# A hybrid attention and mLSTM layer on one core: mLSTM gates, rotation, compressed products and convolution products in another order

## The chip, the core and the metric

The kernel runs as one program on one core of a Trainium2 chip. The metric is the time on the device in microseconds, the median over runs: lower is better. TensorE does the products, VectorE, ScalarE and GpSimd the rest; each engine takes its instructions strictly in its own order and waits for the others by semaphores.

## The reference

One decoder layer on 512 tokens of width 1024 in float32. After an RMS norm `h`, one product with `w_in` (1024 x 5408) gives the inputs of two token mixers. The part that matters here:

```python
z = h @ w_in
q_a, kc_a, vc_a, ks_a, vs_a, kw_a, vw_a, gate_a, qk_b, v_b, o_b, if_b, merge = split(z)
# attention: rotation of the first 16 of 64 components of q and k; three branches
out = concat([t1 * cos - t2 * sin, t2 * cos + t1 * sin, rest])          # partial_rope
kc, vc = compress(kc_a), compress(vc_a)      # 31 overlapping blocks of 32 tokens: gelu(flat @ w1) @ w2
o = g0 * attn(q, kc, vc) + g1 * attn(q, ks, vs) + g2 * attn(q, kw, vw)  # 8 heads, 2 key groups, causal
# mLSTM: convolution over 4 tokens and SiLU on q and k, gates i and f
qk = silu(b + sum_j w[j] * qk_b shifted by j)
lf = log_sigmoid(f);  bcum = cumsum(lf);  m = running maximum of (bcum[t] - bcum[s] + i[s])
h_t = (sum_s exp(bcum[t] - bcum[s] + i[s] - m) (q_t k_s) v_s) / max(|den|, exp(-m))
x = x + (sigmoid(g_a) * (y_a @ w_pa) + sigmoid(g_b) * (y_b @ w_pb)) @ w_out
```

A mixture of experts, a gated embedding and a last norm follow; the change does not touch them.

## The kernel before, in words

All products are split in float32r: a weight piece (128 x 1024, streamed by SyncE) is cast on ScalarE (`whWS`, L103), and the rest is taken on VectorE (`wlWS`, L106), which is the low split; TensorE then does the three products high by high, high by low and low by high. Inside the attention a piece is split at column 640: VectorE does 640, GpSimd 384 (L108); elsewhere VectorE does it all. The rows of a TensorE instruction are named `tp` for transposes, `mm`, `S` and `o` for products.

The stages ahead of the end, with the times of the profiled execution: norm and first products (0 to 38 us); the z1 stage (38 to 91 us), which makes queries, keys, values, gates (`gi`) and the compressed blocks; the attention (to 262 us), woven with the products of the mLSTM; then the mLSTM with the products of `merge` (L979, named z3 here), the output products and the experts.

In the z1 stage the list `ORDER` says in which order pieces come: z4 (288 columns: keys, values and all gates), z0 and z1 (queries), c0 and c1 (the compressed blocks' products, L623, of `bhl` with `w_ck1` and `w_cv1`). What must follow a piece is a generator (`z1_out`: rotate, split into `qs`, transpose at L544 into `qst`; `cmp_out`: gelu, second product). Generators stand in the list `later`, and `advance` steps each of them when its time (`WAIT`) is up. At the end, `while later: advance()` empties it. `cmp_in` makes the blocks' input: the sum `tb` (L614) and the split `bhl` (L615, L616), in two tiles of their own. `rope` (L505) has five VectorE operations: two products with `cos`, two with `nsin` and `sin`, one sum (L511 to L515).

After it come the mLSTM's gates (L733 to L793), some 40 VectorE operations on tiles of 4 to 128 columns: forget gates as a logarithm (ScalarE's table for Ln is loaded at L749), prefix sums by two products on TensorE (L763, L765), maxima by a scan between transposes, and the table `UB` of exponents.

Then the attention: `attention_steps` goes through 32 units (4 query blocks, 4 head pairs, 2 branches). `unit_a` does the scores (L875), the maximum on VectorE (L876), the exponential on ScalarE (L880), the scaling on GpSimd (L886). Two units later `unit_t` transposes (L896) and splits (`ph` L899, `pl` L900), and `unit_pv` multiplies with the values (L912, L917). `cmp_a` (L829) does the scores of the compressed blocks up to `pc` (L850), `cmp_b` its transposes (L857). Between these steps, `weave` takes from `z2_steps` as many products as `FILL_A` says for a query block: first eight channels of the convolution's q and k (24 products of 512 columns each, L802, with four VectorE operations each at L809 and L812), then four channels of v and o (96 products of 256 columns, L292). When these are used up, no more come before the mLSTM's stage.

Instructions are recorded in the order of the text, and a scheduler then sets the order on each engine; nothing is moved while it runs.

Of the kernel before, what the change touches and what calls it, by code (L numbers as in the profile page):

```python
# [19 lines left out]
P = 128  # L20
# [112 lines left out]
def tile_hybrid(ctx, tc, x, p, positions, g_mix, w_in, b_if, w_ck1, w_ck2, pe_ck, w_cv1, w_cv2, pe_cv,  # L133
# [186 lines left out]
    with tc.tile_pool(name="start", bufs=1) as sp:  # L320
# [58 lines left out]
        with in_order():  # L379
# [81 lines left out]
            A.activation(trig[:, 0:2], red.rearrange("p c (b j) -> p c b j", b=NB), AF.Sin)  # L461
            last_g = G.tensor_scalar(trig[:, 2], trig[:, 0], -1.0, None, op0=OP.mult)
# [14 lines left out]
        sin, cos, nsin = trig[:, 0], trig[:, 1], trig[:, 2]  # L477
# [131 lines left out]
    def cmp_in(kv):  # L609
        tb = zp.tile([P, 16, 62], F32, name="tb", bufs=1)  # L610
# [15 lines left out]
    def cmp_out(kv):  # L626

# [107 lines left out]
    with tc.tile_pool(name="gates", bufs=1) as gp:  # L735
        tri = gp.tile([P, 2, P], F32, name="tri")
# [24 lines left out]
        lf2 = lf.rearrange("p b h -> p (b h)")  # L761
        ps = PA.tile([P, 512], F32, name="tp")
# [63 lines left out]
    def attention_steps(ap):
# [135 lines left out]
    with tc.tile_pool(name="att", bufs=1) as ap:  # L962
        weave(attention_steps(ap), z2_steps(ap))
# [764 lines left out]
```

## Time and profile before

| | |
|---|---|
| median of 3 runs | 707.13 us (704.98 to 707.24) |
| profiled execution, its own time | 707.7 us |
| its span in the trace | 705.9 us |
| busy: TensorE, VectorE, ScalarE, GpSimd | 684.4, 561.5, 434.5, 139.1 us |
| granted clock of TensorE, mean | 0.998 |

Busy time of TensorE holds an instruction's whole length, while the next may have started; two starts in a row tell more of how fast it goes. Idle time in brackets stands with what ended it.

### The profile page before, as it was taken

What the parts mean: (1) busy time and instruction counts of PE and PEld (TensorE: products, weight loads), DVE (VectorE), ACT (ScalarE), POOL (GpSimd) and SP (SyncE); (2) the same over time, 40 slices, a digit from 0 to 9 for tenths busy, and PEclk for the clock granted to TensorE, in tenths of its full rate; (3) what the DMA queues carried; (4) which work ended last, traced back from release to release, by engine and by line L of the source; (5) the groups of instructions that cost most, each with busy time, mean ns of one, the idle gap of its engine ahead of it and who ended that gap; (6) DMA issues with size and microseconds to landing.
All of it is one profiled execution on the core that took longest, in us unless ns stands there. A gap on an engine that the chain in (4) does not pass through costs nothing.

```text
span 705.9 us, 11369 instructions
## 1 busy us (share of the span) xinstructions
PE 684.4 (97%) x3813; PEld 579.5 (82%) x3813; DVE 561.5 (80%) x1430; ACT 434.5 (62%) x848; POOL 139.1 (20%) x189
## 2 busy tenths in 40 slices
PE   8999989999999999999999999999999999999995
PEld 5889967789999998888888888876788888887784
DVE  5768988888768668878775763768999999986986
ACT  5547756576556765665453242236999999987642
POOL 5510033234334210000000002122222222110000
PEclk9999999999999999999999999999999999999999
DMA  8435631222212113232229348945999989507511
GB/s 290 110 96 151 168 100 37 84 61 61 61 31 59 32 40 82 61 91 64 86 63 354 121 124 284 372 150 189 384 386 374 370 299 364 234 30 265 194 61 61
DMA packets 81992, 113.72 MB, mean 161 GB/s; under 512 B 9417, under 2 KB 49945, under 8 KB 81930
## 3 DMA queue, kind: packets, MB, share of 16 engines
q1 hardware_dynamic: 72322, 97.14, 41.5%
q0 software_dynamic: 5648, 11.53, 4.5%
q10 hardware_dynamic: 3960, 4.29, 1.8%
q8 instruction: 31, 0.51, 0.3%
q14 instruction: 31, 0.25, 0.1%
HBM read 108.41 MB, written 12.58 MB: 171 GB/s over the span
## 4 chain that ended last, share of the span: by engine, by line
PE 74%; DVE 8%; DMA 7%; ACT 4%; issue 4%; POOL 3%; ACTq 0%; SPq 0%; POOLq 0%; DVEq 0%
PE S L1510 12%; PE mm L979 12%; PE mm L292 7%; PE mm L1682 6%; PE mm L1535 6%; PE mm L1151 6%; PE mm L802 3%; PE mm L1315 3%; PE tp L896 2%; DMA wr<-in_w_re 2%; PE S L875 2%; PE tp L1496 2%; DVE wlWS L106 2%; PE mm L912 1%; ACT whWS L103 1%
## 5 line engine op out<-in xcount | busy, mean ns | idle before, releaser
L106 DVE TENSOR_TENSOR wlWS<-rawWR,whWS 128x1024 fp32r<-128x1024 f32 (+3 forms) x75 | 85.9, 1153 | 25.5 <-ACT whWS L103 24.6
L103 ACT ACTIVATE whWS<-rawWR 128x1024 fp32r<-128x1024 f32 (+1 forms) x76 | 79.1, 1049 | 35.7 <-PE tp L1223 7.0
L106 DVE TENSOR_TENSOR wlWS<-rawWE,whWS 128x1024 fp32r<-128x1024 f32 x58 | 69.2, 1222 | 3.6 <-ACT whWS L103 2.3
L103 ACT ACTIVATE whWS<-rawWE 128x1024 fp32r<-128x1024 f32 x58 | 60.6, 1071 | 5.1 <-PE S L1510 4.1
L292 PE MATMUL mm<-wlWS,hTh 128*128 128x256 f32 (+1 forms) x184 | 54.2, 295 | 0.1
L292 PE MATMUL mm<-whWS,hTl 128*128 128x256 f32 (+1 forms) x184 | 54.2, 294 | 0.0
L292 PE MATMUL mm<-whWS,hTh 128*128 128x256 f32 (+1 forms) x184 | 53.9, 293 | 0.0
L979 PE MATMUL mm<-hTh,whWS 128*128 128x512 f32 x128 | 50.3, 393 | 0.0
L886 POOL TENSOR_SCALAR pr<-pr,sm 128x128 f32<-128x128 f32 (+3 forms) x64 | 34.7, 554 | 78.7 <-DVE sm L884 34.8
L979 PE MATMUL mm<-hTh,wlWS 128*128 128x512 f32 x128 | 50.0, 391 | 0.0
L979 PE MATMUL mm<-hTl,whWS 128*128 128x512 f32 x128 | 50.0, 391 | 0.0
L1510 PE MATMUL S<-whWS,tgh 128*128 128x512 f32 x120 | 48.6, 405 | 0.0
L1510 PE MATMUL S<-wlWS,tgh 128*128 128x512 f32 x120 | 47.8, 398 | 0.0
L1510 PE MATMUL S<-whWS,tgl 128*128 128x512 f32 x120 | 47.3, 395 | 0.0
L880 ACT ACTIVATE pr<-pr,sm 128x128 f32<-128x128 f32 (+3 forms) x64 | 35.4, 555 | 17.0 <-DVE sm L878 16.8
L899 ACT ACTIVATE ph<-tp 128x512 fp32r<-128x512 f32 (+1 forms) x48 | 25.1, 522 | 20.3 <-PE tp L896 19.8
L108 POOL TENSOR_TENSOR wlWS<-rawWR,whWS 128x384 fp32r<-128x384 f32 (+1 forms) x17 | 25.2, 1484 | 62.0 <-ACT whWS L103 57.1
L292 PEld LDWEIGHTS mm<-wlWS,hTh 128*128 128x128 f32 x184 | 34.9, 190 | 0.4 <-DVE wlWS L106 0.3
L292 PEld LDWEIGHTS mm<-whWS,hTl 128*128 128x128 f32 x184 | 34.9, 190 | 0.1
L292 PEld LDWEIGHTS mm<-whWS,hTh 128*128 128x128 f32 x184 | 34.9, 190 | 0.0
L1540 POOL DMA_INDIRECT y_dram<-ye,gidx x16 | 20.8, 1302 | 62.1 <-ACT aeh L1524 59.0
L876 DVE CUSTOM_DVE_ANT_0 pr<-S,strip 128x128 f32<-128x128 f32 (+3 forms) x64 | 29.3, 485 | 3.9 <-PE S L875 3.4
(492 smaller groups left out, 2076.8 us busy)
## 6 DMA issues: line engine op xcount, KB each, us to landing
rawWE<-in_w_e SPq DMA_DIRECT2D x59, 512.0 KB, 9.1
rawWR<-in_w_in SPq DMA_DIRECT2D x40, 512.0 KB, 3.9
mT<-in_w_e SPq DMA_DIRECT2D x22, 512.0 KB, 10.5
rawWR<-in_w_e SPq DMA_DIRECT2D x13, 512.0 KB, 10.1
rawWR<-in_w_out SPq DMA_DIRECT2D x8, 512.0 KB, 4.0
yy<-y_dram SPq DMA_DIRECT2D x8, 512.0 KB, 5.1
rawWR<-in_w_ck SPq DMA_DIRECT2D x4, 512.0 KB, 4.4
rawWR<-in_w_cv SPq DMA_DIRECT2D x4, 512.0 KB, 5.6
```

The costliest lines, as they stand in the source:

```text
L103: self.last_hi = self.nc.scalar.activation(h[:, :n], flat, AF.Copy)
L106: self.last = self.nc.vector.tensor_tensor(l[:, :c], flat[:, :c], h[:, :c].bitcast(F32), OP.subtract)
L108: self.nc.gpsimd.tensor_tensor(l[:, c:n], flat[:, c:], h[:, c:n].bitcast(F32), OP.subtract)
L292: T.matmul(dst[b], a[:, kk, b * P:(b + 1) * P], w[:, kk - k0, :n], start=(kk == 0 and i == 0 and b % share == 0), stop=(kk == NK - 1 and i ...
L876: V.tensor_tensor_reduce(pr[:, hh, :n], s_[:, :n], strip[:, 512 - q0:640], 0.125, -3.0e38, OP.add, OP.max, sm[:, 0, hh:hh + 1])
L880: A.activation(pr[:, hh, :n], pr[:, hh, :n], AF.Exp, bias=sm[:, 1, hh:hh + 1], accum_out=sm[:, 2, hh:hh + 1])
L886: G.tensor_scalar(pr[:, hh, :n], pr[:, hh, :n], sm[:, 3, hh:hh + 1], 1.0, op0=OP.mult, op1=OP.mult)
L979: T.matmul(ps, w[:, k], a[:, k], start=(k == 0 and i == 0), stop=(k == NK - 1 and i == 2))
L1151: T.matmul(ps, w[:, k, f * P:(f + 1) * P], a[:, k], start=(k == 0 and i == 0), stop=(k == 3 and i == 2))
L1510: T.matmul(ps, a[:, 2 * m + k], w[:, k], start=(m == 0 and k == 0 and i == 0), stop=(m == 3 and k == 1 and i == 2))
L1535: T.matmul(acc[c], a[:, k], w[:, 0, c * 512:(c + 1) * 512], start=(k == 0 and i == 0), stop=(k == 1 and i == 2))
L1682: T.matmul(acc, a[:, k], w[:, 0, lo:hi], start=(k == 0 and i == 0), stop=(k == NK - 1 and i == 2))
```

## The change

1. `ORDER`: the third piece of z4 comes before the first of c0, three pieces of c0 stand together, and z1 is last.
2. `rope`: a table `rot` holds cos twice and sin with both signs (four GpSimd operations); two products with it over 16 components and one sum of the swapped halves.
3. `bhl` and `tb` get no tiles of their own; they lie in the parts of `qst` and `oB` that are free so long. `w2d` is copied in `cmp_out`.
4. The convolution's pool is opened early, and `z2_steps` (`fill`) starts while `later` is emptied: seven steps (`FLUSH`) ahead of each step of a generator.
5. The gates are a generator of four steps, `gate_steps`, that `z2_steps` advances at every eighth step of the products of `vo` from the second channel on; `behind` ties each recorded instruction to the last one before it on its engine.
6. `cmp_b` comes one unit later.

```diff
-ORDER = "z4 z4 c0 z4 c0 c0 z0 c0 z0 c1 z1 c1 z1 c1 c1".split()
+ORDER = "z4 z4 z4 c0 c0 c0 z0 c0 z0 c1 z1 c1 c1 c1 z1".split()
+FLUSH = 7
...
     def rope(z, j, heads, pool):
...
-        V.tensor_tensor(a[..., 0:8], z[..., 0:8], tab(cos), OP.mult)
-        V.tensor_tensor(a[..., 8:16], z[..., 8:16], tab(cos), OP.mult)
-        V.tensor_tensor(b[..., 0:8], z[..., 8:16], tab(nsin), OP.mult)
-        V.tensor_tensor(b[..., 8:16], z[..., 0:8], tab(sin), OP.mult)
-        V.tensor_tensor(z[..., 0:16], a, b, OP.add)
+        for i in range(2):
+            V.tensor_tensor(ab[:, i].rearrange("p (b h e) -> p b h e", b=2, h=heads), v,
+                            rot[:, i, 2 * j:2 * j + 2, None, :].to_broadcast([P, 2, heads, 16]), OP.mult)
...
+        for q in range(1 if joint else 2):
+            to = v.rearrange("p b h e -> p (b h) e") if joint else v[:, q]
+            V.tensor_tensor(halves(to, 0), halves(c[:, 0, q], 0), halves(c[:, 1, q], 1), OP.add)
...
-    bhl = zp.tile([P, 16, P], F32R, name="bhl", bufs=1)
+    bhl = qst[:, 4:8].rearrange("p h (m n) -> p (h m) n", n=P)
...
-        tb = zp.tile([P, 16, 62], F32, name="tb", bufs=1)
+        tb = oB.rearrange("p b n -> p (b n)")[:, 0:992].rearrange("p (m n) -> p m n", n=62)
...
-    with tc.tile_pool(name="gates", bufs=1) as gp:
+    def gate_steps(gp):
+        room = gp.tile([P, S], F32, name="cy", bufs=2)
...
-                for _ in tok_mm_steps(dst, 4 * h, 4 * h + 4, wh, wl, 256, 2):
+                for n, _ in enumerate(tok_mm_steps(dst, 4 * h, 4 * h + 4, wh, wl, 256, 2)):
+                    if c and n % 8 == 0:
+                        with behind():
+                            next(gates, None)
                     yield
...
-    while later:
-        advance()
+    fill = z2_steps(conv)
+    while later:
+        for w in list(later):
+            for _ in range(FLUSH):
+                next(fill)
+            if next(w[1], later) is later:
+                later.remove(w)
...
-                    else:
-                        cmp_b(i)
                     yield FILL_C[br - 1]
+                elif pair == 1 and br == 1:
+                    cmp_b(i)
...
-        weave(attention_steps(ap), z2_steps(ap))
+        weave(attention_steps(ap), fill)
```

Three places in the order. VectorE around the low split of z0's first piece (before: the only `wlWS` row here; `khh` and `kll` are keys, `gi` the gates):

```order
108 L580 TENSOR_TENSOR v_461<-mm,v_461 128x2x64
109 L515 TENSOR_TENSOR kz<-rope_a,rope_b 128x4x16
110 L106 TENSOR_TENSOR wlWS<-rawWR,whWS 128x1024
111 L594 CAST khh_456<-tp 64x2x256 x2
112 L585 TENSOR_TENSOR qs<-kz,qs 128x2x2x64
113 L596 CAST kll_457<-tp 64x2x256 x2
114 L580 TENSOR_TENSOR v_461<-S,v_461 128x2x64
```

and after the change, where the row of the same split is the last one (L614 is now L640, L594 is L621, L596 is L623, L106 is L107):

```order
94 L640 TENSOR_TENSOR oB<-TT,cols 128x16x31 x2
95 L621 CAST khh_460<-tp 64x2x256 x2
96 L612 TENSOR_TENSOR qs<-kz,qs 128x2x2x64
97 L623 CAST kll_461<-tp 64x2x256 x2
98 L607 TENSOR_TENSOR v_465<-S,v_465 128x2x64
99 L529 TENSOR_TENSOR rope_ab<-kz,rot 128x64 x2
100 L697 TENSOR_SCALAR gi<-gi 128x4x24
101 L540 TENSOR_TENSOR kz<-rope_ab 128x4x16
102 L107 TENSOR_TENSOR wlWS<-rawWR,whWS 128x1024
```

The split stood ahead of the casts `khh` and `kll`; now it stands behind them, behind a rotation and behind the scaling of `gi`.

TensorE at the last transposes of the queries before (L544; L649 is the second product of the compressed blocks, L802 the convolution):

```order
414 L623 MATMUL o<-whWS,bhl 128x256
415 L623 MATMUL o<-wlWS,bhl 128x256
416 L649 MATMUL S<-gT,w2d 128x64 x2
417 L544 MATMUL tp<-ident,qs 128x128 x8
418 L802 MATMUL mm<-hTh,whWS 128x512
419 L802 MATMUL mm<-hTl,whWS 128x512
420 L544 MATMUL tp<-ident,qs 128x128 x4
421 L802 MATMUL mm<-hTh,wlWS 128x512
422 L544 MATMUL tp<-ident,qs 128x128 x4
423 L802 MATMUL mm<-hTh,whWS 128x512
424 L544 MATMUL tp<-ident,qs 128x128 x4
425 L802 MATMUL mm<-hTl,whWS 128x512
```

and after (L544 is now L571, L802 is L830):

```order
414 L307 MATMUL S<-wlWS,hTh 128x256
415 L571 MATMUL tp<-ident,qs 128x128 x8
416 L830 MATMUL mm<-hTh,whWS 128x512
417 L830 MATMUL mm<-hTl,whWS 128x512
418 L830 MATMUL mm<-hTh,wlWS 128x512
419 L571 MATMUL tp<-ident,qs 128x128 x4
420 L830 MATMUL mm<-hTh,whWS 128x512
421 L830 MATMUL mm<-hTl,whWS 128x512
422 L571 MATMUL tp<-ident,qs 128x128 x4
423 L830 MATMUL mm<-hTh,wlWS 128x512
424 L830 MATMUL mm<-hTh,whWS 128x512
```

The compressed products ahead of the transposes are gone from here, and convolution products stand between the transposes; 35 of them stand ahead of the first scores.

TensorE in the last steps of the attention before (L896 transposes, L912 products with values, L292 products of `vo`):

```order
1403 L912 MATMUL mm<-ph,v_460 128x256
1404 L912 MATMUL mm<-pl,v_460 128x256
1405 L912 MATMUL mm<-ph,v_460 128x256
1406 L912 MATMUL mm<-pl,v_460 128x256
1407 L896 MATMUL tp<-ident,pr 128x128 x4
1408 L292 MATMUL mm<-whWS,hTl 128x256
1409 L292 MATMUL mm<-wlWS,hTh 128x256
1410 L292 MATMUL mm<-whWS,hTh 128x256
1411 L292 MATMUL mm<-whWS,hTl 128x256
1412 L292 MATMUL mm<-wlWS,hTh 128x256
1413 L292 MATMUL mm<-whWS,hTh 128x256
```

and after (L896 is now L937, L912 is L953, L979 is L1021):

```order
1398 L937 MATMUL tp<-ident,pr 128x128 x4
1399 L953 MATMUL mm<-ph,v_464 128x256
1400 L1021 MATMUL mm<-hTh,whWS 128x512
1401 L953 MATMUL mm<-pl,v_464 128x256
1402 L953 MATMUL mm<-ph,v_464 128x256
1403 L953 MATMUL mm<-pl,v_464 128x256
1404 L937 MATMUL tp<-ident,pr 128x128 x4
1405 L953 MATMUL mm<-ph,v_464 128x256
1406 L1021 MATMUL mm<-hTl,whWS 128x512
1407 L953 MATMUL mm<-pl,v_464 128x256
1408 L953 MATMUL mm<-ph,v_464 128x256
```

The eight products of `vo` between a step's transposes and its neighbour's products are gone, and one product of z3 stands in a step.

## Rows read from the trace of the kernel before

**Rows 1.** The summary of the page: busy time, share of the span and instructions of each engine.
```profile
PE 684.4 (97%) x3813; PEld 579.5 (82%) x3813; DVE 561.5 (80%) x1430; ACT 434.5 (62%) x848; POOL 139.1 (20%) x189
```

**Rows 2.** The table by stage (stretch and its length in us, busy time of each engine with its instructions, TensorE's granted clock, DMA share, GB/s).
```profile
91.00:106.00 15.00, 14.12 (x82) 11.04 (x79) 13.15 (x49) 8.37 (x17) 3.94 (x2) 1.00 0.31 88
106.00:120.00 14.00, 13.21 (x75) 9.83 (x73) 12.96 (x59) 9.35 (x31) 4.46 (x10) 1.00 0.15 39
120.00:140.00 20.00, 18.68 (x103) 15.59 (x103) 16.47 (x54) 11.23 (x30) 6.33 (x12) 1.00 0.28 79
140.00:160.00 20.00, 20.00 (x117) 17.51 (x117) 17.37 (x54) 13.97 (x33) 7.97 (x11) 1.00 0.19 54
160.00:180.00 20.00, 19.66 (x145) 18.37 (x144) 18.23 (x53) 12.05 (x28) 8.01 (x11) 1.00 0.22 57
180.00:200.00 20.00, 20.00 (x164) 19.80 (x163) 13.03 (x47) 12.90 (x35) 5.60 (x9) 1.00 0.18 50
```

**Rows 3.** TensorE in order of time, three places of the z1 stage; columns: start us, us, engine, line, operation, out<-in (partitions x elements, type), count, and in brackets the idle time before with its releaser.
```profile
50.01 0.29 PE L292 MATMUL mm<-whWS,hTl 128*128 128x288 f32 x1
51.58 0.39 PE L623 MATMUL o<-whWS,bhl 128*128 128x256 f32 x1 [1.27 <-DVE bhl L616]
...
57.14 0.28 PE L292 MATMUL mm<-whWS,hTh 128*128 128x256 f32 x1
...
62.90 0.28 PE L623 MATMUL o<-whWS,bhl 128*128 128x256 f32 x1
63.44 0.39 PE L623 MATMUL o<-wlWS,bhl 128*128 128x256 f32 x1 [0.26 <-DVE wlWS L106]
...
64.50 0.28 PE L292 MATMUL mm<-whWS,hTl 128*128 128x256 f32 x1
64.91 0.39 PE L292 MATMUL mm<-wlWS,hTh 128*128 128x256 f32 x1
```

**Rows 4.** TensorE in order of time at the last transposes of the queries, at the first scores and at `cmp_b`; columns as in rows 3.
```profile
88.58 0.56 PE L649 MATMUL S<-gT,w2d 128*128 128x64 f32 x4
90.68 1.09 PE L544 MATMUL tp<-ident,qs 128*128 128x128 f32 x8 [1.55 <-DVE qst L549]
...
104.50 0.39 PE L802 MATMUL mm<-hTl,whWS 128*128 128x512 f32 x1
105.40 0.33 PE L875 MATMUL S<-khh,qst 128*128 128x128 f32 x1 [0.51 <-DVE sm L876]
...
137.52 0.39 PE L802 MATMUL mm<-hTl,whWS 128*128 128x512 f32 x1
138.85 0.44 PE L857 MATMUL tp<-ident,pc 128*128 128x128 f32 x2 [0.94 <-DVE pc L850]
```

**Rows 5.** VectorE in order of time around the low split of z0's first piece; columns as in rows 3.
```profile
55.92 1.21 DVE L106 TENSOR_TENSOR wlWS<-rawWR,whWS 128x1024 fp32r<-128x1024 f32 x1
57.15 1.28 DVE L594 CAST khh<-tp 64x512 fp32r<-64x512 f32 x2
58.47 0.42 DVE L585 TENSOR_TENSOR qs<-kz,qs 128x256 fp32r<-128x256 f32 x1
58.90 0.69 DVE L596 CAST kll<-tp 64x512 fp32r<-64x512 f32 x1
```

**Rows 6.** VectorE in order of time: a rotation operation (L511) alone, a part of a split, a rotation operation beside GpSimd's part of it; the first and the last of 22 gate operations; L850 twice. Columns as in rows 3.
```profile
85.52 0.22 DVE L511 TENSOR_TENSOR rope_a<-zt,trig 128x64 f32<-128x64 f32 x1
...
87.00 0.82 DVE L106 TENSOR_TENSOR wlWS<-rawWR,whWS 128x640 fp32r<-128x640 f32 x1 [0.53 <-ACT whWS L103]
87.75 1.05 DVE L511 TENSOR_TENSOR rope_a<-zt,trig 128x64 f32<-128x64 f32 x1
...
98.34 0.18 DVE L768 COPY bc<-tp 128x16 f32<-128x16 f32 x1 [0.48 <-PE tp L763]
...
103.06 0.17 DVE L787 TENSOR_TENSOR ct<-tp,mp 128x16 f32<-128x16 f32 x1
...
138.38 0.42 DVE L850 TENSOR_TENSOR pc<-pc,r 128x256 f32<-128x256 f32 x1
...
177.20 1.24 DVE L850 TENSOR_TENSOR pc<-pc,r 128x256 f32<-128x256 f32 x1
```

**Rows 7.** GpSimd in order of time: its parts of low splits; columns as in rows 3.
```profile
87.05 2.62 POOL L108 TENSOR_TENSOR wlWS<-rawWR,whWS 128x384 fp32r<-128x384 f32 x2 [31.21 <-ACT whWS L103]
...
176.51 1.65 POOL L108 TENSOR_TENSOR wlWS<-rawWR,whWS 128x384 fp32r<-128x384 f32 x1 [0.58 <-ACT whWS L103]
```

**Rows 8.** ScalarE in order of time: a load of its function table; columns as in rows 3.
```profile
94.45 1.28 ACT L635 ACT_TABLE_LOAD   x1
```

**Rows 9.** TensorE in order of time in the last steps of the attention (eight products of L292 from 259.17 to 260.08); columns as in rows 3.
```profile
258.81 0.60 PE L896 MATMUL tp<-ident,pr 128*128 128x128 f32 x4
259.17 0.36 PE L292 MATMUL mm<-whWS,hTl 128*128 128x256 f32 x1
...
260.08 0.28 PE L292 MATMUL mm<-wlWS,hTh 128*128 128x256 f32 x1
260.20 0.28 PE L912 MATMUL mm<-ph,v 128*128 128x256 f32 x1
```

**Rows 10.** ScalarE in the same step.
```profile
259.45 0.60 ACT L899 ACTIVATE ph<-tp 128x512 fp32r<-128x512 f32 x1 [1.27 <-PE tp L896]
```

**Rows 11.** VectorE in the same step.
```profile
260.08 0.69 DVE L900 TENSOR_TENSOR pl<-tp,ph 128x512 fp32r<-128x512 f32 x1 [1.18 <-ACT ph L899]
```

More of the change, by code (lines that the diff above doesn't have):

```diff
@@ L267, in in_order, with behind @@
             last[i.engine] = i
+    @contextmanager
+    def behind():
+        cur = nc.cur_bb
+        traced = cur.bb.instructions
+        n = len(traced)
+        last = {i.engine: i for i in traced}
+        yield
+        assert nc.cur_bb is cur
+        for i in traced[n:]:
+            if i.engine in last:
+                tc.add_manual_dep(i, last[i.engine].name, mybir.DependencyInfo(
+                    mybir.DependencyClass.NoSync, mybir.DependencyReason.DATA), reason="behind")
     ident = const.tile([P, P], F32, name="ident")
@@ L334, in tile_hybrid @@
         bif = const.tile([P, 8], F32, name="bif")
+        rot = const.tile([P, 2, NB, 16], F32, name="rot")
         def square(b):
@@ L460, in tile_hybrid @@
             z4w.append(st.get(("z", 4, 1)))
-            A.activation(trig[:, 0:2], red.rearrange("p c (b j) -> p c b j", b=NB), AF.Sin)
-            last_g = G.tensor_scalar(trig[:, 2], trig[:, 0], -1.0, None, op0=OP.mult)
+            A.activation(trig, red, AF.Sin)
+            tr4 = trig.rearrange("p c (b j) -> p c b j", b=NB)
+            for s_ in range(2):
+                G.tensor_copy(rot[:, 0, :, 8 * s_:8 * s_ + 8], tr4[:, 1])
+                last_g = G.tensor_scalar(rot[:, 1, :, 8 * s_:8 * s_ + 8], tr4[:, 0], (1.0, -1.0)[s_], None, op0=OP.mult)
             zz_mm(3, 0, (0, 2, 1))
@@ L626, in cmp_out @@
     def cmp_out(kv):
+        if kv == 0:
+            V.tensor_copy(w2d, w2s[:, 0, :, None, :].to_broadcast([P, 2, 2, 64]))
         u = zp.tile([P, 256], F32, name="gelu_u", bufs=1)[:62]
@@ L734, in tile_hybrid @@
     UB = const.tile([P, 4, NB, NB], F32, name="UB")
-    with tc.tile_pool(name="gates", bufs=1) as gp:
-        tri = gp.tile([P, 2, P], F32, name="tri")
+    def gate_steps(gp):
+        room = gp.tile([P, S], F32, name="cy", bufs=2)
+        tri = room[:, 0:2 * P].rearrange("p (a b) -> p a b", a=2)
         G.memset(tri, 1.0)
@@ L761, in tile_hybrid @@
         lf2 = lf.rearrange("p b h -> p (b h)")
+        yield
         ps = PA.tile([P, 512], F32, name="tp")
@@ L769, in tile_hybrid @@
         V.tensor_tensor(u0, fi[:, :, 0:4], bc, OP.subtract)
+        yield
         ps3 = PA.tile([P, 512], F32, name="tp")
         T.transpose(ps3[:16, :P], u0.rearrange("p b h -> p (b h)"), ident)
-        ut = gp.tile([16, P], F32, name="ut")
+        ut = room[:16, 2 * P:3 * P]
         V.tensor_copy(ut, ps3[:16, :P])
-        cm = gp.tile([16, P], F32, name="cm")
+        cm = room[:16, 3 * P:]
         V.tensor_tensor_scan(cm, ut, ut, -3.0e38, OP.max, OP.max)
+        yield
         ps4 = PA.tile([P, 512], F32, name="tp")
@@ L796, in z2_steps @@
     def z2_steps(wp):
+        gates = gate_steps(wp)
         for c in range(8):
@@ L824, in z2_steps @@
                              AF.Copy if c < 2 else AF.Tanh, scale=1.0 if c < 2 else 0.5)
+    fill = z2_steps(conv)
[5 more added lines that the diff above has]
+                later.remove(w)
+    zp_c.__exit__(None, None, None)
+    tt_ctx.__exit__(None, None, None)
     def attention_steps(ap):
```

19 lines of the change are left out of this document (10 added, 9 removed).

## The prediction

> **What bounds the kernel now.** I read the summary first, then the table by stage, then TensorE's own rows in order of time where it stalls, then the engines it waits for. TensorE is busy 97% of the span [rows 1]. In the table by stage it is without a gap at 140-160 us and at 180-200 us; its idle time near this change lies ahead of that, and at 91-140 us VectorE is nearly as full as TensorE [rows 2]. Busy time hides part of the loss: a 256-column product shows 0.28 us, but the next one starts 0.12 us later. So I count stalls from start to start. The large ones are: 50.01 to 51.58 before the first compressed product, which waits for `bhl`; 62.90 to 63.44 and 64.50 to 64.91, which wait for a low split [rows 3]; 88.58 to 90.68 before the queries' transposes; 104.50 to 105.40 at the first scores; 137.52 to 138.85 before the transposes of `cmp_b` [rows 4]. Behind the attention, at 262 us, the products of z3 stand ready, so I let what is lost or won before it reach the end whole. 0.3% of this kernel is 2.1 us, about what a measurement of it can tell from no change. No large product is added or taken away: TensorE's work is the same, and the question is only where it stands still.
>
> **1. Compressed products later, the queries' first piece behind them.** In the order after, 13 products of z4 and 8 transposes stand between the place of the first stall and the first compressed product. By the old rows `bhl` came at 51.5, and those 21 pieces last beyond it. So the stall goes, 1.57 less a usual step of 0.13: -1.44. The pieces from the stall to z0 (8, 13, 8 and 16 of them) took from 51.58 to 57.14 [rows 3], 5.56 us, and they are the same ones after the change; TensorE now begins them at 50.13 and stands at z0's first piece at 55.7. The low split of this piece, which VectorE began at 55.92 and ended at 57.13 [rows 5], is now queued behind two casts `khh` (1.28), one `qs` (0.4), two casts `kll` (1.3), a `v`, a rotation and the scaling of `gi` (0.6 together, at the lengths of their kind): 3.6 us later, an end at 60.7. TensorE has 1.0 us of work that needs no low split (four products, four transposes, one compressed product) and would idle from 56.7 to 60.7. So the new wait lies between 0 (if the casts' inputs come much sooner) and 4.0 (the plain sum); I take **+3.0**, nearer the plain sum, since the order is fixed and only its start can move. Behind it four splits stand together ahead of TensorE, so the two later stalls go: -0.42 and -0.29. The step in all: +0.85 (from -2.15 to +1.85).
>
> **2. Convolution products between the transposes, rotation in three operations.** The stall at 88.58 is 2.10 us, of which the four small products take some 0.4: 1.7 lost. The transposes wait for `qst`, which on VectorE stands behind two rotation operations, the first of 1.05 us where such a one takes 0.22 [rows 6]; meanwhile GpSimd did its parts of two splits, 1.31 us each [rows 7]. In the order after, these two splits are whole on VectorE: +0.4 us each there (1.21 against 0.82 [rows 5, 6]), but GpSimd is out of the way, the rotation has three operations, and TensorE has 3, 2, 16 and 7 products of 0.23 us between the transposes and 7 behind them. So I take the 1.7 as gone. The stall at 104.50 (0.90 less a step of 0.23) goes too, since the 22 gate operations which VectorE did between 98.34 and 103.23 with a few others among them [rows 6] no longer stand ahead of the first scores. Between the two, gaps of 0.2 to 0.4 stand among the transposes; I take 1.4 us for these, since VectorE has 1.85 us to spare of 15 there now [rows 2] and the gate operations' 3.5 (22 of about 0.16) more after. Step: **-3.8** (from -1.7, the first stall alone, to -4.5).
>
> **3. Early attention.** At 106-120 us VectorE is busy 12.96 of 14 us, and TensorE idles 2.1 us at 106-140 [rows 2]. The convolution's first channel is done earlier, and so are VectorE's operations for it; the transposes of `cmp_b` come a unit later, which frees 1.33 less 0.23, 1.1 us. With some 1.3 of the small gaps: **-2.4** (from 0, if other waits fill the place, to -3.5).
>
> **4. Gates in the attention.** Some 40 small VectorE operations (the 22 in 3.5 us, and 17 of 0.17 ahead of them: about 6.3 us), and the two table loads (1.28 us for one [rows 8]), now fall into about 17 us at the change from the second to the third query block. There the convolution is over in the order after. By the nearest stretch of old without it, 180-200, VectorE would have 5.9 us free in 17; by 160-180, the same query blocks, 1.5 [rows 2]. So it lacks between 0.4 and 4.8 us. ScalarE has room for the loads (12 to 14 of 20 busy). A unit's result is needed two units later, which covers most of a lack that is made up soon: **+1.1** (0 to +4). `pc` takes 0.42 us alone and 1.24 while GpSimd's split of 1.65 us runs [rows 6, 7], like the rotation in step 2. [...]
>
> **5. A tail without fill.** Thirty-five products are used early, so those of `vo` run out between the last two pairs of scores. The last seven transpose steps of the attention have three products of z3 among them, where each had 6 to 8 products of 0.12 us. Such a step is 0.36 us of transposes (258.81 to 259.17) and 0.48 of products on TensorE [rows 9], 0.84 in all. But the transposes of a step stand behind the products of the step two before, and these behind a chain: transposes 0.60, `ph` 0.60, `pl` 0.69, products 0.48 [rows 9 to 11], 2.4 us for two steps, 1.2 for one. Seven times 0.36 is 2.5, less 0.7 for the three z3 products of 0.23: **+1.8** (0.5, if a chain overlaps the next one better than that, to 4.5, if the scores' own chain of reduction, exponential and scaling ends last).
>
> Sum: 0.85 - 3.8 - 2.4 + 1.1 + 1.8 = -2.45. The profiled execution took 707.7 us (span 705.9), 0.6 over the median of 707.13 of the runs shown. Against its own time the sum gives 705.25, against the median **704.7**.
>
> **The rivals.**
> *Gates and tail cost more than the transposes give (slower).* One mechanism: VectorE is late in the middle of the attention. Its price: each of GpSimd's splits in the stretch holds a two-input operation 0.8 us longer (1.24 against 0.42 [rows 6]), three of them 2.4 us; as VectorE has none to spare, TensorE waits, and step 4 is its upper end, +4; the tail, where VectorE's chain is again last, is +3.5. The sum is then +2.15: 709.3. It decides once VectorE is behind by more than the lead of two units, some 5 us. For it: the rows of 1.24 and 1.05. Against: most gate operations are short, and no TensorE work waits for them at once. Chance 0.24.
> *The new waits are covered (much faster).* The low split of z0 is there when TensorE comes, and the tail costs 1.0: -2.45 - 3.0 - 0.8 = -6.25, 700.9. For it: the split was just in time before. Against: its place in the order. Chance 0.15.
> *The stalls only change place (no change).* VectorE's work is the same but for some 2 us of rotation; step 3 gives nothing, and the sum is about 0: 707. The moved copy `w2d` does nothing at all, for it stands in the same early place in both orders. For it: VectorE is full around every stall [rows 2]. Chance 0.21.
>
> **How the numbers follow.** My forecast has 0.40, with 702.5 to 706.5 as its own range. Faster by over 0.3%: the second rival 0.15, the forecast's part below 705.0, 0.27, and 0.03 of the third: 0.45. Slower: the first rival but for 0.03, and 0.01 of the third: 0.22. Within 0.3%: the rest, 0.33. The range takes in the second rival's time with 1 us below it and the first's with 1 us above: 699.9 to 710.3.
>
> **What would show it.** Step 1: a wait of TensorE for `wlWS` at about 57 to 60 us. Step 2: none for `qst` at 88, and first scores that start 3 us or more ahead in relation to the work done by then. Step 3: none for `pc`. Step 4: waits beside the gates' rows, and gate rows of several times 0.17. Step 5: idle TensorE in the last 10 us of the attention, with `pl` as releaser. The working is wrong if no wait stands at 57 us, if the tail idles less than 0.5 us, or if TensorE loses time behind 262 us.

## The result: 10 us slower

| | before | after |
|---|---|---|
| median of the runs on one chip | 706.68 us (704.98 to 707.24) | 716.98 us (715.18 to 717.79) |
| profiled execution: own time, span, mean granted clock | 707.7, 705.9, 0.998 | 717.79, 716.1, 0.986 |

The ratio is 1.0146, interval 1.0119 to 1.0174. Three executions far above all others (839.0 us of e11, 957.2 of the kernel before, 1723.8 of e6) are left out of all ratios. The forecast of 704.7 and its range to 710.3 are both missed, on the side of the first rival but beyond its 709.3.

Against [rows 1] the summary of the changed kernel shows TensorE with 8 us more busy time and no product more, and digits of 8 in the row of its clock, where before has only 9s:

```profile
PE 692.4 (97%) x3813; PEld 584.7 (82%) x3813; DVE 559.8 (78%) x1412; ACT 434.6 (61%) x848; POOL 136.1 (19%) x190
...
PEclk9998999999899999999999999999999999999998
```

The table by stage (columns: busy time and count for PE, PEld, DVE, ACT, POOL, then granted clock, DMA share, GB/s) places them, and answers to [rows 2]; narrower stretches stand in the second fence:

```profile
50.00:62.00 12.00, 8.55 (x56) 7.70 (x55) 10.92 (x23) 10.30 (x26) 0.00 (x0) 0.79 0.19 52
62.00:76.00 14.00, 14.00 (x113) 14.00 (x112) 11.42 (x20) 8.01 (x14) 0.00 (x0) 0.93 0.74 219
...
140.00:160.00 20.00, 19.72 (x106) 16.73 (x106) 16.11 (x50) 12.80 (x32) 5.55 (x8) 0.94 0.13 41
...
180.00:200.00 20.00, 19.63 (x135) 19.18 (x136) 14.95 (x60) 9.44 (x23) 5.52 (x8) 0.83 0.10 27
```
```profile
60.00:62.00 2.00, 2.00 (x9) 1.84 (x9) 1.28 (x3) 1.98 (x4) 0.00 (x0) 0.50 0.33 49
...
64.00:66.00 2.00, 2.00 (x19) 2.00 (x19) 1.35 (x2) 0.59 (x1) 0.00 (x0) 1.00 0.90 280
...
137.90:139.00 1.10, 1.06 (x9) 1.06 (x10) 1.10 (x4) 0.00 (x0) 0.00 (x0) 1.00 0.23 15
139.00:142.40 3.40, 3.40 (x11) 2.67 (x11) 2.86 (x9) 1.88 (x6) 0.00 (x0) 0.50 0.47 149
...
180.00:184.00 4.00, 3.79 (x17) 3.79 (x18) 1.10 (x7) 1.31 (x4) 0.73 (x2) 0.50 0.00 0
```

At 60:62 TensorE is busy for 2.00 of 2 us with 9 products, at 64:66 with 19: at a granted clock of 0.50 the busy column still looks like full work. The count beside it gives it away.

The waits of TensorE from 45 to 275 us (engine, what it did, whom it waited for: sum, times, longest). Those of before for `bhl`, for `qst` and, at 138 us, for `pc` [rows 3, 4] are gone; these stand in their place:

```profile
PE S L875 <- DVE sm L917: 3.7, 2, 2.2
PE tp L617 <- DVE kll L623: 2.3, 1, 2.3
PE o L649 <- ACT whWS L104: 1.1, 1, 1.1
PE o L953 <- DVE pl L941: 1.0, 2, 0.6
PE tp L898 <- issue: 0.9, 1, 0.9
```

The last of them is a wait for `pc` too, at the transposes of `cmp_b` for the first query block. The profile names no releaser for it, but it ends at 114.84, and VectorE's last operation on `pc` at 114.74:

```profile
114.84 0.41 PE L898 MATMUL tp<-ident,pc 128*128 128x128 f32 x2 [0.88 <-issue]
```
```profile
114.33 0.41 DVE L891 TENSOR_TENSOR pc<-pc,r 128x256 f32<-128x256 f32 x1
```

**Where the 10 us arise.** The table below is worked out from TensorE's start times: each matmul is valued at the median start-to-start step of its form in before, and the sums are compared; a cell says how much later (+) a kernel's profiled execution reaches the sum that before has at that time. Differences between two lines belong to the stretch between them. Zero products that an experiment adds count nothing.

| before at | after | e1 | e2 | e3 | e5 | e7 | e8 | e9 |
|---|---|---|---|---|---|---|---|---|
| 48 us | -1.3 | -2.1 | -1.5 | -1.5 | -1.7 | 0.1 | -1.0 | -1.0 |
| 78 | 2.8 | -2.2 | 3.3 | 3.0 | -1.7 | 3.9 | 4.2 | -1.1 |
| 102 | -0.4 | -5.3 | 0.6 | -0.2 | -4.8 | 0.7 | 1.0 | -4.0 |
| 138 | -3.1 | -8.4 | -0.6 | -2.9 | -3.8 | -2.0 | -1.3 | -6.4 |
| 150 | 0.1 | -7.0 | -0.3 | 0.3 | -3.4 | 1.2 | -2.0 | -6.0 |
| 174 | -0.1 | -7.1 | 0.0 | 0.2 | -3.1 | 1.0 | -0.2 | -6.5 |
| 192 | 4.7 | -5.0 | -0.7 | 1.6 | -3.8 | 3.1 | 1.3 | -4.3 |
| 252 | 5.5 | -4.3 | -0.2 | 2.4 | -3.3 | 3.9 | 2.1 | -3.0 |
| 264 | 8.4 | -1.2 | 2.7 | 5.3 | -0.1 | 6.7 | 2.1 | 0.3 |
| 400 | 10.0 | 0.4 | 4.3 | - | 1.5 | 8.3 | 3.6 | 1.9 |

So the changed kernel loses 4.0 at 48 to 78, wins 5.9 to 138, and loses 3.2 at 138 to 150 (place B), 4.8 at 174 to 192 (place C) and 2.9 at 252 to 264 (the tail); the rest is small pieces.

**Place A**, TensorE in order of time, then VectorE (start, duration, engine, line, operation, [idle before <- who ended it]):

```profile
54.79 0.28 PE L307 MATMUL mm<-whWS,hTl 128*128 128x256 f32 x1
57.38 0.44 PE L617 MATMUL tp<-ident,qs 128*128 128x128 f32 x1 [2.31 <-DVE kll L623]
...
59.60 0.58 PE L649 MATMUL o<-whWS,qst 128*128 128x256 f32 x1 [1.14 <-ACT whWS L104]
60.16 0.58 PE L307 MATMUL mm<-wlWS,hTh 128*128 128x256 f32 x1
60.54 0.42 PE L307 MATMUL mm<-whWS,hTh 128*128 128x256 f32 x1
60.76 0.42 PE L307 MATMUL mm<-whWS,hTl 128*128 128x256 f32 x1
...
63.75 0.36 PE L307 MATMUL mm<-whWS,hTh 128*128 128x256 f32 x1
63.94 0.28 PE L307 MATMUL mm<-whWS,hTl 128*128 128x256 f32 x1
64.06 0.28 PE L307 MATMUL mm<-wlWS,hTh 128*128 128x256 f32 x1
```
```profile
54.77 1.28 DVE L621 CAST khh<-tp 64x512 fp32r<-64x512 f32 x2
...
56.54 1.30 DVE L623 CAST kll<-tp 64x512 fp32r<-64x512 f32 x2
...
58.89 1.22 DVE L107 TENSOR_TENSOR wlWS<-rawWR,whWS 128x1024 fp32r<-128x1024 f32 x1
```

The low split comes at 58.89 where before had it at 55.92 [rows 5], and z0's first product that needs it starts at 60.16, 0.05 after its end. The profile puts the two waits down to other things: the transposes wait for `kll`, the compressed product for a cast on ScalarE. But the product at 60.16 could not have come before the split's end without them either. Up to 63.75 the next ones follow 0.21 us apart, from 63.94 on 0.12: the clock fell in the wait (1.00 from 54 to 57 us, 0.51 from 57 to 60.1) and stayed down 3.6 us after it. A step of 0.21 in place of 0.12 is 1.6 us in that time.

**Place B**, TensorE: the next scores of the compressed keys, as the second query block begins, wait for the maxima (`sm`, L917) of two units before, on VectorE among the convolution's last operations (0.74 us each, L837). TensorE, then VectorE:

```profile
137.94 0.86 PE L875 MATMUL S<-kcm,qst 128*128 128x64 f32 x6 [1.52 <-DVE sm L917]
...
141.87 0.63 PE L830 MATMUL mm<-hTl,whWS 128*128 128x512 f32 x1
142.30 0.45 PE L830 MATMUL mm<-hTh,wlWS 128*128 128x512 f32 x1
142.59 0.39 PE L830 MATMUL mm<-hTh,whWS 128*128 128x512 f32 x1
142.82 0.40 PE L830 MATMUL mm<-hTl,whWS 128*128 128x512 f32 x1
```
```profile
136.81 0.74 DVE L837 SCALAR_TENSOR_TENSOR cy<-mm,cols,cy 128x511 f32<-128x511 f32 x1
137.47 0.41 DVE L917 CUSTOM_DVE_ANT_0 pr<-S,strip 128x256 f32<-128x256 f32 x1
```

Here the clock is still full behind the wait; it falls at 139.0, 1.1 us after its end. Products of 512 columns then stand 0.43 apart until 142.30 and 0.23 behind: 3.4 us at the lower level, 1.6 of them lost.

**Place C**, TensorE, ScalarE, VectorE, each in order of time:

```profile
180.21 0.85 PE L875 MATMUL S<-kcm,qst 128*128 128x64 f32 x3 [2.22 <-DVE sm L917]
...
186.56 0.39 PE L307 MATMUL mm<-whWS,hTl 128*128 128x256 f32 x1
186.77 0.29 PE L307 MATMUL mm<-wlWS,hTh 128*128 128x256 f32 x1
186.90 0.28 PE L307 MATMUL mm<-whWS,hTh 128*128 128x256 f32 x1
```
```profile
172.51 1.28 ACT L773 ACT_TABLE_LOAD   x1
...
176.85 1.28 ACT L921 ACT_TABLE_LOAD   x1 [1.80 <-DVE sm L919]
```
```profile
179.27 0.17 DVE L923 RECIPROCAL sm<-sm 128x2 f32<-128x2 f32 x1 [1.41 <-ACT pr L921]
...
179.59 0.56 DVE L917 CUSTOM_DVE_ANT_0 pr<-S,strip 128x384 f32<-128x384 f32 x1
```

Read backwards: TensorE needs the score buffer that the maxima of 179.59 free; VectorE stood 1.41 us in front of them in a reciprocal that needs the exponentials; ScalarE was at a table load of 1.28 us ahead of them, at the exponentials' line, 4.3 us after the one at the line of the gates' Ln. The clock then stays down to 186.56, 6.4 us, of which 2.8 are lost (0.213 a step in place of 0.12). At the three places together TensorE works 13.4 us at a granted clock of 0.50 and loses 6.0 by these steps. An estimate from the clock alone, half of the 13.4 us, is 6.7; the steps in the rows give 0.7 less. At A and C the clock was down when the next product started (0.51 from 57 to 60.1, 0.50 from 180 to 184); at B it fell only 1.1 us after the wait's end.

The **tail**, TensorE, which answers to [rows 9]:

```profile
263.98 0.39 PE L953 MATMUL o<-pl,v 128*128 128x256 f32 x1 [0.64 <-DVE pl L941]
```

### The profile page after: what moved, and what is told of

It reads as the page before. It is cut to its first block, busy times and chain, and to the rows that moved or that the text cites. A ratio compares the mean times of both kernels' runs of the same rounds, so it can differ in the third digit from the quotient of the medians.

```text
span 716.1 us, 11333 instructions
## 1 busy us (share of the span) xinstructions
PE 692.4 (97%) x3813; PEld 584.7 (82%) x3813; DVE 559.8 (78%) x1412; ACT 434.6 (61%) x848; POOL 136.1 (19%) x190
## 5 line engine op out<-in xcount | busy, mean ns | idle before, releaser
L107 DVE TENSOR_TENSOR wlWS<-rawWR,whWS 128x1024 fp32r<-128x1024 f32 (+2 forms) x75 | 85.6, 1151 | 32.2 <-ACT whWS L104 31.5
L104 ACT ACTIVATE whWS<-rawWR 128x1024 fp32r<-128x1024 f32 (+2 forms) x76 | 79.0, 1048 | 40.8 <-PE tp L1265 11.7
L107 DVE TENSOR_TENSOR wlWS<-rawWE,whWS 128x1024 fp32r<-128x1024 f32 x58 | 69.2, 1221 | 3.7 <-ACT whWS L104 2.3
L307 PE MATMUL mm<-whWS,hTh 128*128 128x256 f32 (+1 forms) x184 | 55.8, 304 | 0.0
L307 PE MATMUL mm<-wlWS,hTh 128*128 128x256 f32 (+1 forms) x184 | 55.8, 304 | 0.0
L1021 PE MATMUL mm<-hTh,whWS 128*128 128x512 f32 x128 | 50.8, 397 | 0.0
L1021 PE MATMUL mm<-hTl,whWS 128*128 128x512 f32 x128 | 50.6, 395 | 0.0
L1021 PE MATMUL mm<-hTh,wlWS 128*128 128x512 f32 x128 | 50.5, 394 | 0.0
L921 ACT ACTIVATE pr<-pr,sm 128x128 f32<-128x128 f32 (+3 forms) x64 | 35.4, 555 | 16.6 <-DVE sm L919 16.5
L307 PEld LDWEIGHTS mm<-wlWS,hTh 128*128 128x128 f32 x184 | 36.4, 198 | 0.4 <-DVE wlWS L107 0.3
L307 PEld LDWEIGHTS mm<-whWS,hTh 128*128 128x128 f32 x184 | 36.5, 198 | 0.1
L307 PEld LDWEIGHTS mm<-whWS,hTl 128*128 128x128 f32 x184 | 36.4, 198 | 0.1
L917 DVE CUSTOM_DVE_ANT_0 pr<-S,strip 128x128 f32<-128x128 f32 (+3 forms) x64 | 29.4, 486 | 3.7 <-PE S L916 3.1
L109 POOL TENSOR_TENSOR wlWS<-rawWR,whWS 128x384 fp32r<-128x384 f32 (+1 forms) x15 | 19.8, 1320 | 64.2 <-ACT whWS L104 64.1
```

Source lines behind the costliest of these rows:

```text
L104: self.last_hi = self.nc.scalar.activation(h[:, :n], flat, AF.Copy)
L107: self.last = self.nc.vector.tensor_tensor(l[:, :c], flat[:, :c], h[:, :c].bitcast(F32), OP.subtract)
L307: T.matmul(dst[b], a[:, kk, b * P:(b + 1) * P], w[:, kk - k0, :n], start=(kk == 0 and i == 0 and b % share == 0), stop=(kk == NK - 1 and i ...
L917: V.tensor_tensor_reduce(pr[:, hh, :n], s_[:, :n], strip[:, 512 - q0:640], 0.125, -3.0e38, OP.add, OP.max, sm[:, 0, hh:hh + 1])
L921: A.activation(pr[:, hh, :n], pr[:, hh, :n], AF.Exp, bias=sm[:, 1, hh:hh + 1], accum_out=sm[:, 2, hh:hh + 1])
L1021: T.matmul(ps, w[:, k], a[:, k], start=(k == 0 and i == 0), stop=(k == NK - 1 and i == 2))
```

## The experiments

The theory: three new waits cost their length, and a good part of the loss is the clock that falls in or behind them. The rivals: GpSimd, working beside VectorE, makes the gates slow, or plain waiting is all. Line numbers are those of each kernel. Ratios are to the kernel before on the same chip, with their interval.

**e1: everything but `ORDER`.** The list of before is put back.

```diff
-ORDER = "z4 z4 z4 c0 c0 c0 z0 c0 z0 c1 z1 c1 c1 c1 z1".split()
+ORDER = "z4 z4 c0 z4 c0 c0 z0 c0 z0 c1 z1 c1 z1 c1 c1".split()
```

> The changed kernel with the list ORDER of before, all else changed. [...] Rival (the first wait costs only its own 4 us and gives 2.2 back, as forecast; the loss lies in VectorE, late beside GpSimd in the attention): 1 to 2 us faster, 715 to 716.

Measured: 710.88 us (708.07 to 712.04), ratio 1.009, 1.0074 to 1.0107; about 713 was expected. Place A has no wait and no lower clock; the old stall is back, and 48 to 78 us cost 0 where they cost 4.0: the new `ORDER` makes A (which part of it, e9 shows). At B it waits 1.26 us, the clock stays, and 138 to 150 costs 1.4 in place of 3.2. Its profiled execution was its fastest (708.07, clock 0.997); the others lay at 710.8 to 712.0 with clocks of 0.992 to 0.994, and where the clock fell in those no trace tells. At place C it has the same wait as the changed kernel, and yet the clock stays (TensorE, then the stretch behind it):

```profile
173.15 0.52 PE L875 MATMUL S<-kcm,qst 128*128 128x64 f32 x3 [2.17 <-DVE sm L917]
```
```profile
174.00:178.00 4.00, 4.00 (x37) 4.00 (x36) 2.75 (x8) 3.21 (x7) 2.04 (x3) 1.00 0.00 0
```

The stretch 174 to 192 costs 2.1 there and 4.8 in the changed kernel. The difference, 2.7, is what the row steps gave for the clock at C, 2.8.

**e2: the gates back ahead of the attention.**

```diff
...
-        gates = gate_steps(wp)
...
-                for n, _ in enumerate(tok_mm_steps(dst, 4 * h, 4 * h + 4, wh, wl, 256, 2)):
-                    if c and n % 8 == 0:
-                        with behind():
-                            next(gates, None)
+                for _ in tok_mm_steps(dst, 4 * h, 4 * h + 4, wh, wl, 256, 2):
...
+    with tc.tile_pool(name="gates", bufs=1) as gp:
+        for _ in gate_steps(gp):
+            pass
```

> The changed kernel with the gates' operations recorded between the flush and the attention, as before. Theory: the wait at 178 us and its half clock go, 4.8 us, and 1 to 1.5 us are lost at the first scores: about 713.5, and TensorE at full clock at 176-190 us. Rival (the wait at 178 us is the phase of the units, not of the gates): 717 or later, with a wait for S near the first scores of the third block as before.

Measured: 711.9 us (711.43 to 712.81), ratio 1.0096, 1.0079 to 1.0112. Place C is gone (174 to 192: -0.7, clock 1.00), so it needs the gates there. B is gone as well (0.3). Of the 5.9 won at 78 to 138, 3.9 are left: the gates' absence there is worth 2.0.

**e3: no logarithm, hence no table loads for it.** The question is whether the loads make VectorE, and with it TensorE, late at C. The forget gates' logarithm is replaced by a copy times zero. The gate values change and the later stages with them (5493 matmuls for 3813), so only the trace up to the end of the attention is read, not the 4074.81 us in all.

```diff
-        A.activation(lnw, w1p, AF.Ln)
+        A.activation(lnw, w1p, AF.Copy, scale=0.0)
```

> The changed kernel, whose logarithm is replaced by a multiplication with zero on the same engine at the same place: the forget gates' correction by the logarithm is left out of the result. Orders of TensorE and VectorE stay nearly the same, and only ScalarE's two table loads in the attention go. [...] Rival (the 40 small operations on VectorE, lengthened beside GpSimd, make it late): within 1 us of the changed kernel, the wait at 178 us still there.

Measured: TensorE's order is that of the changed kernel. All gate operations are still on VectorE, four of them earlier in its order; the 37 take 8.7 us in all, where they take 8.0 in the changed kernel and 6.8 in before. The wait at C falls from 2.2 to 1.2, the stretch 174 to 192 from 4.8 to 1.4, and the clock stays:

```profile
179.83 0.52 PE L875 MATMUL S<-kcm,qst 128*128 128x64 f32 x3 [1.22 <-DVE sm L917]
```

So the loads are 1.0 us of the wait. The 1.2 that are left go only with the gates (e2); whether their number makes them or their lengthening beside GpSimd, no run separates. And of the 3.4 won, 2.7 are the clock, which in e1 and e7 stays with the whole wait too.

**e4 and e7: zero products in the wait of A.** They add nothing to the sum and need no low split; 36 of them in e4, 54 in e7. The question is whether the clock stays up where TensorE does not stand still.

```diff
...
+                    if b == 0 and kk == k0 and i == 2:
+                        for _ in range(zero_n.pop() if zero_n else 0):
+                            T.matmul(dst[b], zer, w_hi(wh, n), start=False, stop=False, skip_group_check=True)
...
+                zero_n.append(36)
```

> The changed kernel with 36 more products of 256 columns on TensorE, with a zero stationary matrix, that add nothing, in the wait at 55 us. [...]

Measured for e4: 716.28 us (714.45 to 719.23), ratio 1.0151, 1.0131 to 1.0171; 715.2 was expected. Inconclusive: the split came at 61.2, 2.00 us of wait were left, and the clock fell 1.2 us behind it.

> e4_zero with 54 instead of 36 products with a zero matrix, 6.4 us of them, so that TensorE has no idle time over 0.5 us at 55-61 us. Theory (idle time lowers the clock): no fall of the clock at 55-68 us, z0's products 0.12 us apart, 1 to 2 us less than the changed kernel although 6.4 us of work were added. Rival (another cause): the clock falls there as in e4_zero, no gain.

Measured for e7: 714.87 us (712.97 to 716.44), ratio 1.0107, 1.0068 to 1.0146. With 54 products more that is not above the changed kernel's 716.98; the intervals of the two ratios overlap, so a gain in time is not settled. TensorE, then the stretch behind it:

```profile
56.04 6.29 PE L316 MATMUL mm<-whWS,zer 128*128 128x256 f32 x54
62.16 0.28 PE L317 MATMUL mm<-wlWS,hTh 128*128 128x256 f32 x1
62.28 0.28 PE L317 MATMUL mm<-whWS,hTh 128*128 128x256 f32 x1
```
```profile
62.00:64.00 2.00, 2.00 (x19) 2.00 (x19) 1.61 (x3) 1.31 (x3) 0.00 (x0) 1.00 0.49 107
```

The first product with the low split comes 2.0 us later than in the changed kernel (62.16 for 60.16). 1.4 of that e7 is late already at 48 us. The split itself ends 0.2 later in the stretch, and the zero products overrun it by 0.5; also, TensorE's order differs there, so that the 0.6 us of pieces which the changed kernel does in the wait come behind it. Still 48 to 78 costs no more (3.8 for 4.0), as what follows runs 0.12 apart from the start. So some 1.5 are won, near the 1.6 that the steps gave for the clock at A. That the clock has a price at A is shown; its size rests on these sums. Most of the difference between the two profiled executions, though, is made at C. There TensorE's order is the same again, and so is the wait of 2.22 us, but the clock stays at 1.00 and the stretch costs 2.1:

```profile
181.32 0.52 PE L887 MATMUL S<-kcm,qst 128*128 128x64 f32 x3 [2.22 <-DVE sm L929]
```

**e5: `ORDER` and gates both back.**

> The changed kernel with both the ORDER and the place of the gates of before; what is left of the change are the rotation in three operations, the convolution products between the transposes, the shared tiles and the transposes of the compressed scores a unit later. Theory (the waits at 55 and 178 us come from these two parts alone, and the tail without fill from the early products): TensorE is some 4 us ahead of the kernel before at 240 us, loses 3 in the tail and 1 behind it: 704 to 706 where the kernel before takes 705. Rival (the early products themselves cost, since the units of the first blocks then run into VectorE): 708 or more, with waits at 100-170 us.

Measured: 709.7 us (708.06 to 711.35), ratio 1.0054, 1.0035 to 1.0073. That is the rival's time. Neither A nor C is there, and at 102 us it leads by 4.8; 1.4 is given back by 150, 3.2 in the tail, 1.6 between 264 and 400. At 122.8, 0.8 us behind a wait of 0.86 (for `pr`, L926), its clock falls for 3.4 us.

**e6: e5 with less fill in the first two query blocks**, so that products of `vo` are left for the tail.

```diff
-FILL_A = 12.0, 10.3, 6.8, 7.2
+FILL_A = 9.8, 8.1, 6.8, 7.2
```

> e5_both with 9.8 and 8.1 instead of 12.0 and 10.3 fill products a unit in the first two query blocks, so that the products of vo last to the end of the attention again. Theory (the tail's loss is the missing fill): the 3 us of the tail are won, and with as few new waits in the first two blocks as VectorE's rows allow 1 or 2 are lost: 702 to 704. Rival (fill only moves the waits: what is taken from the first blocks is missed there): same time as e5_both, with the waits at 100-170 us instead of 255-265.

Measured: 708.19 us (fastest 705.86), ratio 1.0026, 1.0009 to 1.0043. The tail costs 0.6 in place of 3.2, but 2.4 of its lead are lost at 120 to 138. As e5 loses about as much there, in part by its clock, it is not settled that the first blocks want the fill as well.

**e8: no products between the transposes.**

```diff
-FLUSH = 7
+FLUSH = 0
```

> The changed kernel with FLUSH = 0: no convolution products are put between the steps that empty the list, and the products of vo last longer. Theory (early products win 3 to 4 us at 88-105 and their lack costs 3 in the tail): the tail's waits go, waits at 86-105 us come back, so within 2 us of the changed kernel; the wait at 136 us, which is a matter of how channel and block fall together, goes or moves. Rival (the early products are what loses): 4 us or more faster.

Measured: 710.35 us (709.74 to 711.29), ratio 1.0055, 1.0039 to 1.0071, some 6.4 us under the changed kernel: not within 2, as expected, but beyond the rival's 4. The tail is gone (252 to 264: 0.0), so step 5 names its cause rightly. And 78 to 138 still wins 5.5 of the 5.9: the early products themselves give 0.4. Place B turns into a gain of 0.7, and C costs 1.5 with the clock at 1.00, as the waits now fall elsewhere; A costs 5.2 (clock 0.50 from 60 to 66).

**e9: the low split ahead of the casts.** One number makes z4's followers wait longer, and the split of z0's first piece then stands ahead of `khh` and `kll` on VectorE.

```diff
-WAIT = 4, 13, 11.5
+WAIT = 4, 17, 11.5
```

> The changed kernel with one number of WAIT, 13, set to 17, so that the keys' transposes and casts are recorded behind z0's first piece; in the order VectorE's low split of that piece then stands ahead of the four casts. Theory (the wait at 55 us is that queue): neither the wait nor the fall of the clock at 54-64 us, nor the old wait for the compressed products' input: 6 us less than the changed kernel, ratio to the kernel before 1.005 to 1.007. Rival (the buffers that free late hold the split back): the wait stays over 2 us, and at most 2 us are won.

Measured: 708.04 us (706.46 to 710.44), ratio 1.0034, 1.002 to 1.0048: most of the loss is won back by one number. TensorE waits 1.90 us there, and the clock does not fall:

```profile
57.29 0.39 PE L307 MATMUL mm<-wlWS,hTh 128*128 128x256 f32 x1 [1.90 <-DVE wlWS L107]
```

48 to 78 costs -0.1: the split's place is what A costs. B is gone without an edit there (+0.4); its work now comes 3 us earlier than in the changed kernel, and why that frees it no run tells. C costs 2.2: its wait is only 0.79 us, but 2.4 us behind it the clock falls for 3.4 us. 246 to 270 takes back 5 us.

**e10: e6 with the new `ORDER` and e9's number; e11: e9 with e6's `FILL_A`; e12: e1 with e6's `FILL_A`.** Their edits are those shown.

> e6_fill (gates in their old place, fewer fill products in the first two blocks) with the ORDER of the change and 17 in WAIT. Theory: the wait of 1.3 us for the compressed products' input, that e6_fill still has, goes with no new one: 1 to 2 us less than e6_fill, ratio to the kernel before 0.999 to 1.002. Rival (VectorE, late by the casts, makes the queries' transposes wait): same as e6_fill, 1.003.

> e9_wait17 (the change with 17 in WAIT) with 9.8 and 8.1 instead of 12.0 and 10.3 fill products a unit in the first two query blocks. Theory (of e9's ratio of 1.0034 the tail's lack of fill is the larger part: TensorE is 4.6 us ahead of the kernel before at 246 us and level at 264): the tail is full, and 3 us are won: ratio 0.997 to 1.000. Rival (what is kept for the tail is missed in the first blocks): ratio 1.002 to 1.005, new waits at 105-150 us.

> e1_order (the change with the ORDER of before) with the same smaller fill in the first two blocks. Theory as for e11: e1's profiled execution was 4.3 us ahead at 252 us and level at the end, so 3 us less than e1_order: ratio 1.000 to 1.004, as the wait of the gates' table load stays. Rival: no gain over e1_order, 1.007 to 1.011.

Measured: e10 709.17 us, 1.0048 (1.0029 to 1.0067); e11 707.86 us, 1.0025 (1.0011 to 1.004); e12 707.09 us, 1.0021 (1.0008 to 1.0034). Of e11 only the times are read. e10 is not better than e6, as its rival has it: TensorE still waits 1.8 us for the split, and new waits of up to 1.0 stand at 124 to 168. e11 comes out as its rival has it, and its interval holds e9's ratio, so the fill's share there is not settled. e12 is as expected: against e1 0.7% less, the clearest gain of the smaller fill. In its trace no wait between 160 and 185 us is over 0.4, though the gates and both table loads stand there (173.69 and 177.94), so these alone do not make C; how the units fall together does too. No version beats the kernel before.

## Why the prediction was wrong, point by point

**Step 1**, +0.85 as put, +4.0 as measured (48 to 78). The gone stalls came as forecast: no wait for `bhl`, and 0.8 won back from 60 to 78. The split is late for the reason given, behind two `khh` and two `kll`. But TensorE stood from 55.07 and not from 56.7 on: of the 1.0 us of work that was to come first, the four transposes wait for `kll` themselves and the compressed product for ScalarE's cast, and no wait for `wlWS` is on the page. Of the two ends, 0 and 4.0, I took 3.0; TensorE lost 4.6 (from 54.91, when the next product was due, to 60.16, less 0.6 for the pieces done in it), above the upper end, and e1 and e9 show it to be the split's place. The 1.6 for the clock had no term.

**Steps 2 and 3**, -6.2 as put, -5.9 as measured (78 to 138). The sum is right, in part by luck. Of the three waits, that for `qst` and that at the first scores are gone; `pc` is no longer waited for at 138 us but, against the sign named for step 3, for 0.88 us at 114. The share of the convolution products in the sum is wrong: e8 wins nearly as much without them. The gates' absence gives 2.0 (e2); the rest stays with rotation and order, which no run separates.

**Step 4**, +1.1 with an upper end of 4 as put, +4.8 as measured (174 to 192). The sentence that failed is "ScalarE has room for the loads": it has, as busy share, but a load in front of an exponential holds VectorE's next operation in line and with it TensorE, for 1.0 of the 2.2 us (e3). The plain wait costs 2.1, as e1 and e7 show; 2.7 more is the clock. That VectorE slows down beside GpSimd is seen in the rows: a gate operation takes 0.43 there and `pc` 1.22, with GpSimd at work from 169.64 (0.94 us) and from 185.66 (1.57 us), where the same two of before take 0.19 and, alone, 0.42 [rows 6]. On all 37 gate operations it comes to 1.2 us (8.0 for 6.8).

```profile
169.73 0.43 DVE L765 TENSOR_TENSOR fi<-gi,bif 128x32 f32<-128x32 f32 x1
...
186.29 1.22 DVE L884 TENSOR_TENSOR pc<-pc,r 128x256 f32<-128x256 f32 x1
```

**Step 5**, +1.8 as put (0.5 to 4.5), +2.9 as measured (252 to 264), with `pl` as releaser of the 1.0 us of idle time that the list has there: mechanism right, 1.1 too small, and e8 shows its cause.

**What no step held.** Place B, 3.2, of which 1.6 is the clock: I looked for waits where the gates and transposes moved, not where two sequences of VectorE come to meet later. And the clock itself: 1.6 + 1.6 + 2.8 = 6.0 of the 12.5 us between the sum of the forecast, -2.45, and the 10.1 between the two profiled executions. I valued each stall at its length, from a trace in which none of 1.3 to 1.6 us had lowered the clock [rows 3, 4]. The first rival had the right sign and, for B and C, the right place (VectorE late in the middle of the attention). Its mechanism, operations lengthened beside GpSimd, explains neither A nor the clock; for the 1.2 us of C's wait that e3 keeps it is not excluded.

**Left open.** Which waits lower the clock. It fell in the waits at A (2.31 and 1.14) and at C (2.22, also in e4). It fell 0.7 to 1.8 us behind the 1.5 at B (changed kernel, e3, e4, e7), 1.2 behind the 2.00 in e4, 0.8 behind the 0.86 in e5, 2.4 behind the 0.79 in e9. After 1.90 in e9, 2.17 in e1, 2.22 in e7 and 0.87 in e6 it did not fall, nor after 1.55 before. No run here tests what decides it.

The lag also grows by 1.5 to 1.6 us between 264 and 400 us in all the versions that the table follows so far, with no wait that the list names. A loss behind 262 us was one of the forecast's signs of a wrong working; its cause stays open.

The lead at 48 us, 1.3 in the changed kernel and in no step of the forecast, goes with the moment at which TensorE first starts products of 512 columns 0.23 us apart. Four products of 512 columns in before and in the changed kernel; the product behind them starts at 15.26 and 13.89, which is 0.43 and 0.23 a step:

```profile
13.55 1.91 PE L304 MATMUL mm<-whW,hTl 128*128 128x512 f32 x4
```
```profile
12.96 1.09 PE L319 MATMUL mm<-whW,hTl 128*128 128x512 f32 x4
```

e7, which gets there as late as before does (11 products from 12.7 to 16.5 us, 10 in before, 20 in the changed kernel), has no such lead.

## What to carry to other kernels

A stall of TensorE had two prices here, its length (2.1 us at C in e1 and e7) and the products behind it at a granted clock of 0.50 (2.7 us more at C in the changed kernel); look at the count of products beside a busy time, and at the granted clock, before taking "busy" for work. When an edit moves a cast, a split or a table load, follow the strict order of the engine that it joins to the first instruction that TensorE needs, even where the engine's busy share leaves room. Where an order is set by numbers, try one of them by itself first: here one waiting time won back most of what the change had lost (ratio 1.0034 for 1.0146).

## What the runs showed of the hardware

- Around waits of 1.5 to 2.3 us the clock fell, and TensorE worked 3.6, 3.4 and 6.4 us at a granted clock of 0.50. The same wait of 2.22 us, in the same order, cost 4.8 in the changed kernel's execution and 2.1 in e7's, by the clock alone.
- Useless products cost no time at A: with 54 of them, 6.3 us in a wait of some 5, the clock stayed up there, and the stretch cost 3.8 in place of 4.0.
- The mean clock differs between runs of one kernel: the changed one has 0.986 in its runs of 717.4 and 717.8 us and 0.992 in those of 715.2 and 716.6. It doesn't tell all: e9 has runs of 706.5 us at 0.995 and 708.7 at 0.997.
- A table load took 1.28 us at each place [rows 8]; the changed kernel has two around the gates' logarithm, at its line (172.51) and at the line of the exponentials after it (176.85).
